# A two-layer attention and mixture-of-experts trunk: the first norm's scale and shift moved onto turned rows, pass 0 fed by a product, the expert choice rewritten

## The chip, the cores and the metric

The kernel runs on one core of one Trainium2 chip. The metric is the device time of one execution in microseconds (us). The kernel before took 848.21 us, the median of three runs (848.0 to 849.41).

The core has a matrix engine (PE; its weight loads are shown apart as PEld), a vector engine (DVE), a scalar engine (ACT), GpSimd (POOL), and a queue (SP) that issues most of the DMA transfers. Every engine works through its own list of instructions in order, and waits on semaphores for the others.

## What is computed

512 tokens of width 1024 pass through two layers. Each layer computes an attention part and an output projection, adds the residual, and norms (the first norm); then a router picks two of 16 experts for each token, within one of four groups, and the result of the experts is added and normed again. What matters here is the stretch from the first norm to the experts:

```python
x = layer_norm(DEEPNORM_ALPHA * x + einsum('bsm,md->bsd', mix, w_out[l]), ln1_g[l], ln1_b[l])

def moe_ffn(x, w_router, router_bias, w_gate, w_up, w_down):
    scores = sigmoid(dot(xt, w_router))
    biased = (scores + router_bias).reshape(N, N_GROUPS, EXPERTS_PER_GROUP)     # 4 groups of 4
    group_score = sum(top_k(biased, 2)[0], axis=-1)
    g_sel = argmax(group_score, axis=-1)
    in_group = take_along_axis(biased, g_sel[:, None, None], axis=1)[:, 0]
    _, local = top_k(in_group, 2)
    expert_idx = g_sel[:, None] * EXPERTS_PER_GROUP + local
    w = take_along_axis(scores, expert_idx, axis=1);  w = w / sum(w, axis=-1, keepdims=True)
    gates = sum(one_hot(expert_idx, N_EXPERTS) * w[..., None], axis=1)
    h = silu(einsum('nd,edf->enf', xt, w_gate)) * einsum('nd,edf->enf', xt, w_up)
    return einsum('enf,efd->nd', h * gates.T[:, :, None], w_down)

x = layer_norm(DEEPNORM_ALPHA * x + moe_ffn(x, ...), ln2_g[l], ln2_b[l])
```

## The kernel before

**Who sets the order.** The program is written as many small streams (Python generators, functions whose names begin with `s_`) that a planner, `Flow`, interleaves when the program is built. Each step names an engine and an estimated cost; the planner takes the step that can start first, with a small weight for the stream's priority (`PRIO`). What it fixes is the order of each engine's list. At run time an engine only waits for the data of the next instruction in its list.

**The stretch at stake.** The 512 tokens are four tiles, t = 0 to 3, of 128 rows, held in `X`. The output projection (`s_wout`; its products are L283 to L285) ends with tile 3. For each half tile `s_half` adds the residual and takes statistics (L970, L972). `s_router` turns the tile with PE (L441), ACT copies it (L279), PE multiplies it by the router's weights (L1035), and three small DVE steps make the logits (L1041, L1045, L1046). `s_norm1` applies the norm to `X` with four DVE instructions of 512 columns a tile (two at L990, two at L998), with mean, deviation, gain and shift, and then SP stores the tile in DRAM (`XD`, L1060). `s_choose` works on a pair of tiles (q = 0: tiles 0 and 1; q = 1: tiles 2 and 3): ACT's exponential (L1070), then a chain of small DVE steps from L1080 on (comparisons of all pairs in a group, the best group, ties) that ends in the one-hot choice `ohb` (L1098). `s_rank` counts with PE (L1188 to L1191) at which place of its expert's list each token stands, and builds from that on DVE the operands of one more product (L1195 to L1212). That product, `s_table` (L1221), gives for each pass and slot the row to fetch; DVE writes it as integers (L1225).

**Passes.** Each expert has room for 96 tokens. The 16 x 96 slots are cut into 12 passes of 128. For a pass, POOL gathers its 128 rows from `XD` by an indirect DMA (`s_gather`, L1293), PE turns them with eight transposes (`turn_rows`, L1505), ACT and DVE copy the turned rows out of the banks in two pieces of 512 columns (`s_rows`, through L279 and L280), and PE multiplies them by gate and up weights (`s_passes`, L1596; four products of 32 slots side by side). ACT and DVE make the hidden values (`s_act`, L1474, L1475), PE turns them (L1502) and multiplies them by the down weights (`second`, L1570). Weights are loaded by SP (L1355, L1357, L1361) into slots that the passes set free. All of this is in float32; the trace shows two records for each float32 product that isn't a transpose (64 at L1596 for the 32 of a pass).

**Filler.** From the end of the projection until the planner thinks that the first gather has landed, `s_warm` puts products of a matrix of ones into PE's list (L1124); their result isn't used.

**The end of a layer.** The last two passes stay on chip (`NEAR`); the others' rows go to DRAM and come back (`s_far`). `s_combine` adds them to alpha times `X` and norms. For tiles 0 and 2, `s_alpha` multiplies `X` by alpha on ACT (L1620); for tiles 1 and 3 a product with `ident_alpha` does it (L1675).

Of the kernel before, what the change touches and what calls it, by code (L numbers as in the profile page):

```python
# [6 lines left out]
F32 = mybir.dt.float32  # L7
# [9 lines left out]
P = 128  # L17
D = 1024
# [16 lines left out]
FAR = 8192.0  # L35

# [159 lines left out]
def body(tc, sb, pp, dr, x, w_in, attn_sinks, c_q_norm_g, c_kv_norm_g, w_uq, w_ukv, w_out, ln1_g, ln1_b,  # L196
# [105 lines left out]
    ident_alpha = fixed(P)  # L302
    V.tensor_scalar(ident_alpha, ident, ALPHA, None, op0=OP.mult)
# [16 lines left out]
    desc = fixed(4)  # L320
    V.tensor_scalar(desc, iotf[:, :4], -1.0, float(NE), op0=OP.mult, op1=OP.add)
    lower = fixed(4, 4)
    G.iota(lower, pattern=[[1, 4], [-1, 4]], base=0, channel_multiplier=0, allow_small_or_imprecise_dtypes=True)
    V.tensor_scalar(lower, lower, 0.0, None, op0=OP.is_gt)
# [45 lines left out]
    for key, n in (("sg", 2 * NE), ("zz", 2 * NE), ("bi", 2 * NE), ("c1", 8 * NE), ("c2", 8 * NE), ("g4", 2 * NE), ("rk", 2 * NE), ("gs", 8), ("m1", 8),  # L370
                   ("pick", 8), ("oh", 4 * NE), ("wts", 4), ("posk", 4), ("row", 4), ("eb", 4), ("op", 4 * NP)):
# [107 lines left out]
    def layer(l, xready, prev_free):  # L479
# [542 lines left out]
        def s_router(t):  # L1022
            yield E("gain")
            r0, z = smalls["r0", t], smalls["zz", t // 2][:, t % 2 * NE:(t % 2 + 1) * NE]
            for h in range(2):
# [17 lines left out]
            yield E("stat", t)  # L1043
            mv, rs = smalls["mv", t], smalls["rs", t]
            yield ve(16, lambda: V.scalar_tensor_tensor(r0, gbv[:, 0], mv[:, 0:1], r0, op0=OP.mult, op1=OP.subtract))  # L1045
            e = yield ve(16, lambda: V.scalar_tensor_tensor(z, r0, rs[:, 0:1], gbv[:, 1], op0=OP.mult, op1=OP.subtract))  # L1046
# [8 lines left out]
        def s_norm1(t):  # L1055
            yield E("gb1")
            er = yield E("stat", t)
            e = yield from s_norm(t, (aux.of(F32), gb1), E("stat", t).got, er, None, True)
            flow.set(E("normed", t), e)
            xd = yield dma(524e3, lambda: SY.dma_start(XD[l][t * P:(t + 1) * P, :], X[:, t]), [e])  # L1060
            flow.set(E("xd", t), xd)


        def s_choose(q):
# [5 lines left out]
            t = yield ac(32, lambda: A.activation(sg, smalls["zz", q], AF.Exp), [flow.now])  # L1070
            flow.set(E("exp", q), t)
            C1, C2 = (c.rearrange("p (g a b) -> p g a b", a=4, b=4) for c in (c1, c2))
            b84, G84, R84 = (a.rearrange("p (g a) -> p g a", a=4) for a in (bi, g4, rk))
            other = b84[:, :, None, :].to_broadcast([P, 8, 4, 4])
            own = b84[:, :, :, None].to_broadcast([P, 8, 4, 4])
            gs2, pick2 = (a.rearrange("p (t g) -> p t g", t=2) for a in (gs, pick))

            def v(fn, after=None):
                return ve(60, fn, after)
            yield v(lambda: V.tensor_scalar(sg, sg, 1.0, None, op0=OP.add))  # L1080
# [698 lines left out]
```

## Time and profile before

| | us |
|---|---|
| median of three runs | 848.21 |
| profiled execution, its own time | 847.3 |
| profiled execution, its span | 845.5 |
| PE busy in it | 817.0 (97%) |
| DVE busy | 510.3 (60%) |
| ACT busy | 315.4 (37%) |
| POOL busy | 103.6 (12%) |

The span runs from the first instruction to the last; the 1.8 us around it belong to the execution's own time. Busy time of PE contains the filler products, so it doesn't tell by itself how much of the work of PE is needed. The granted clock of PE was 0.996 over the whole span.

### The profile page before, as it was taken

What the parts mean: (1) busy time and instruction counts of PE and PEld (TensorE: products, weight loads), DVE (VectorE), ACT (ScalarE), POOL (GpSimd) and SP (SyncE); (2) the same over time, 40 slices, a digit from 0 to 9 for tenths busy, and PEclk for the clock granted to TensorE, in tenths of its full rate; (3) what the DMA queues carried; (4) which work ended last, traced back from release to release, by engine and by line L of the source; (5) the groups of instructions that cost most, each with busy time, mean ns of one, the idle gap of its engine ahead of it and who ended that gap; (6) DMA issues with size and microseconds to landing.
All of it is one profiled execution on the core that took longest, in us unless ns stands there. A gap on an engine that the chain in (4) does not pass through costs nothing. (4 is left out here: it accounts for less than half of the span.)

```text
span 845.5 us, 16062 instructions
## 1 busy us (share of the span) xinstructions
PE 817.0 (97%) x6288; PEld 534.9 (63%) x6288; DVE 510.3 (60%) x1504; ACT 315.4 (37%) x790; POOL 103.6 (12%) x135
## 2 busy tenths in 40 slices
PE   7999999999999999999999999999999999999995
PEld 7878896667896333333587889776688843333332
DVE  6799999975591130002998999999458513100157
ACT  4434647973111222122245174677531112212211
POOL 1010102000002111100211001200101111111004
PEclk9999999999999999999999999999999999999998
DMA  8422340174476999997444218010944579999862
GB/s 267 149 79 80 114 169 26 26 258 140 151 275 187 340 373 376 370 362 284 163 105 143 75 51 273 2 52 26 338 160 163 188 272 365 373 367 367 293 270 100
DMA packets 119138, 172.73 MB, mean 204 GB/s; under 512 B 12101, under 2 KB 95557, under 8 KB 119056
## 3 DMA queue, kind: packets, MB, share of 16 engines
q1 hardware_dynamic: 112720, 156.12, 54.1%
q0 software_dynamic: 6336, 15.52, 5.2%
q8 instruction: 51, 0.84, 0.4%
q14 instruction: 31, 0.25, 0.1%
HBM read 154.01 MB, written 25.17 MB: 212 GB/s over the span
## 5 line engine op out<-in xcount | busy, mean ns | idle before, releaser
L283 PE MATMUL bank<-ring,ra 128*128 128x512 f32 (+4 forms) x448 | 167.1, 373 | 0.5 <-ACT fa L605 0.5
L1596 PE MATMUL bank<-fa,ra 128*32 128x512 f32 x1080 | 159.7, 592 | 1.2 <-DVE ra L280 0.7
L284 PE MATMUL bank<-ring,xl 128*128 128x512 f32 (+4 forms) x448 | 157.5, 352 | 0.9 <-DVE xl L452 0.9
L285 PE MATMUL bank<-ring,ra 128*128 128x512 f32 (+4 forms) x448 | 157.9, 352 | 0.0
L279 ACT ACTIVATE fa<-bank 128x512 f32<-128x512 f32 (+3 forms) x170 | 85.5, 517 | 142.5 <-PE bank L441 82.6
L1475 DVE TENSOR_TENSOR fa<-fa,bank 128x256 f32<-128x256 f32 x24 | 10.1, 420 | 200.3 <-ACT fa L1474 200.3
L1596 PEld LDWEIGHTS bank<-fa,ra 128*32 128x32 f32 x1080 | 49.8, 110 | 75.5 <-issue 70.1
L283 PEld LDWEIGHTS bank<-ring,ra 128*128 128x128 f32 x448 | 85.0, 190 | 14.8 <-issue 7.1
L285 PEld LDWEIGHTS bank<-ring,ra 128*128 128x128 f32 x448 | 84.8, 189 | 8.2
L284 PEld LDWEIGHTS bank<-ring,xl 128*128 128x128 f32 x448 | 85.2, 190 | 7.4 <-DVE xl L452 1.3
L1570 PE MATMUL bank<-fa 128*32 128x512 f32 x504 | 80.4, 595 | 1.5 <-DVE fa L280 0.6
L441 PE MATMUL bank<-fa 128*128 128x128 f32 (+1 forms) x456 | 71.5, 281 | 7.4 <-DMA fa<-in_x_dram 5.7
L441 PEld LDWEIGHTS bank<-fa 128*128 128x128 f32 (+1 forms) x456 | 55.1, 143 | 24.4 <-issue 10.5
L474 ACT ACTIVATE ring<-fa 128x1024 fp32r<-128x1024 f32 (+4 forms) x56 | 49.4, 897 | 56.1 <-PE bank L284 49.8
L1596 PE MATMUL bank<-ring,ra 128*32 128x512 f32 x360 | 67.1, 592 | 0.0
L1474 ACT ACTIVATE fa<-bank 128x256 f32<-128x256 f32 x24 | 9.2, 385 | 151.7 <-PE bank L1596 151.7
L475 DVE TENSOR_TENSOR ring<-fa,ring 128x1024 fp32r<-128x1024 f32 (+4 forms) x56 | 58.4, 1051 | 7.8 <-ACT ring L474 7.8
L747 DVE MATCH_REPLACE8 aux<-fa,aux 128x256 f32<-128x256 f32 (+2 forms) x96 | 51.8, 544 | 0.0
L746 DVE MAX8 fa<-aux 128x8 f32<-128x256 f32 (+2 forms) x96 | 50.6, 550 | 0.1
L787 PE MATMUL bank<-fa 64*128 64x256 f32 (+7 forms) x256 | 47.4, 413 | 0.0
L800 ACT ACTIVATE fa<-fa 128x256 f32<-128x256 f32 (+3 forms) x89 | 44.5, 503 | 0.0
L1570 PEld LDWEIGHTS bank<-fa 128*32 128x32 f32 x504 | 19.3, 108 | 35.6 <-issue 34.1
(222 smaller groups left out, 1221.2 us busy)
## 6 DMA issues: line engine op xcount, KB each, us to landing
fa<-in_w_gate_dram SPq DMA_DIRECT2D x45, 512.0 KB
fa<-in_w_up_dram SPq DMA_DIRECT2D x45, 512.0 KB
fa<-in_w_down_dram SPq DMA_DIRECT2D x21, 1024.0 KB
xl<-in_w_down_dram SPq DMA_DIRECT2D x9, 1024.0 KB
fa<-in_w_out_dram SPq DMA_DIRECT2D x8, 1024.0 KB
yd<-fa SPq DMA_DIRECT2D x16, 512.0 KB
ring<-in_w_gate_dram SPq DMA_DIRECT2D x15, 512.0 KB
ring<-in_w_up_dram SPq DMA_DIRECT2D x15, 512.0 KB
```

Of the source, the lines that this page charges most:

```text
L279: return Step([("A", 0.05 + n / 1200, lambda: A.activation(dst, src, AF.Copy)), ("V", 0.12 + n / 960, lambda: V.tensor_copy(dst, src))], a ...
L283: T.matmul(ps, xh, wh, start=start, stop=False)
L284: T.matmul(ps, xl, wh, start=False, stop=False)
L285: T.matmul(ps, xh, wl, start=False, stop=stop)
L441: T.transpose(ps[:n, j, :], s, ident)
L474: yield Step([("A", 0.09 + n / 1200, lambda: A.activation(hv, raw, AF.Copy))], None)
L475: t = yield ve(n, lambda: V.tensor_tensor(lv, raw, hv.bitcast(F32), op=OP.subtract))
L746: yield ve(nk, lambda: V.max(m8, sc))
L747: yield ve(nk, lambda: V.match_replace(sc, m8, sc, MARK))
L787: T.matmul(got[1][:, a * nk:(a + 1) * nk], qs[h], ks[h], start=True, stop=True)
L1570: T.matmul(a[1][cs], ht[:, j, cs], E("raw", e, 2).got[1][:, j, n * 512:(n + 1) * 512], start=j == 0, stop=j == 1)
L1596: T.matmul(acc[1][cs], gh[:, 4 * u + j, cs], E("raw", e, u).got[1][:, j], start=u + j == 0, stop=u + j == 4)
```

## The change

1. **The norm is split.** `s_norm1` now only subtracts the mean and divides by the deviation, in one ACT instruction of 1024 columns a tile. Gain and shift (`gcol`, already there by column for the router) are applied where the rows are turned: `s_rows` copies each of the eight turned blocks of 128 columns with one ACT or DVE instruction that multiplies by the gain and adds the shift. Blocks were copied four at a time before.
2. **Pass 0 by a product.** `s_first` builds for each tile a 128 x 128 matrix that holds a one where a token belongs to a slot of pass 0, and multiplies `X` by it. The sum over the four tiles is the turned rows of pass 0, so pass 0 has no gather and no transposes. `s_warm` fills only until the last of these matrices is there.
3. **The choice by differences.** `s_choose` subtracts all pairs and compares the differences with 0 or with a tiny negative number, once for experts and once for groups. A token that finds no room gets a large place number (`NONE`) in `s_rank`.
4. **The logits.** The two halves of a tile's logits are joined in one DVE step that reads the bank.
5. **The residual's share put late.** `X` needs alpha times gain and shift for the end of the layer. `s_alpha` now does that for all four tiles with four DVE instructions of 512 columns each, after `first`, `table` and the store of the tile. `ident_alpha` becomes `ident`.

The core of the diff (left out: constants, the overflow branch, names):

```diff
@@ s_router
                 else:
-                    e = yield ve(16, lambda: V.tensor_tensor(r0, r0, gp[1][:, :NE], op=OP.add))
+                    tp = e
+                    es = yield E("stat", t)
+                    mv, rs = smalls["mv", t], smalls["rs", t]
+                    e = yield ve(16, lambda: V.scalar_tensor_tensor(r0, gbv[:, 0], mv[:, 0:1], r0, op0=OP.mult, op1=OP.subtract), [es])
+                    e = yield ve(16, lambda: V.scalar_tensor_tensor(r0, r0, rs[:, 0:1], gbv[:, 1], op0=OP.mult, op1=OP.subtract), [e])
+                    e = yield ve(16, lambda: V.scalar_tensor_tensor(z, gp[1][:, :NE], rs[:, 0:1], r0, op0=OP.mult, op1=OP.subtract), [e, tp])
@@ s_norm1
-            yield E("gb1")
             er = yield E("stat", t)
-            e = yield from s_norm(t, (aux.of(F32), gb1), E("stat", t).got, er, None, True)
+            for h in range(2):
+                yield E("seen", h, t)
+            mv, rs = smalls["mv", t], smalls["rs", t]
+            e = yield ve(1, lambda: V.tensor_scalar(rs[:, 1:2], mv[:, 0:1], rs[:, 0:1], -1.0, op0=OP.mult, op1=OP.mult), [er])
+            e = yield ac(D, lambda: A.activation(X[:, t], X[:, t], AF.Identity, scale=rs[:, 0:1], bias=rs[:, 1:2]), [e])
             flow.set(E("normed", t), e)
             xd = yield dma(524e3, lambda: SY.dma_start(XD[l][t * P:(t + 1) * P, :], X[:, t]), [e])
+        def s_alpha(t):
+            yield E("gb1")
+            yield E("first")
+            yield E("table")
+            yield E("xd", t)
+            g, b = aux.of(F32), gb1
+            for h in range(2):
+                cs = slice(h * 512, (h + 1) * 512)
+                yield ve(512, lambda: V.scalar_tensor_tensor(X[:, t, cs], X[:, t, cs], ALPHA, g[:, cs], op0=OP.mult, op1=OP.mult))
+                e = yield ve(512, lambda: V.scalar_tensor_tensor(X[:, t, cs], b[:, cs], ALPHA, X[:, t, cs], op0=OP.mult, op1=OP.add))
@@ s_warm
-            while E("gathered").t is None or flow.free["T"] < E("gathered").t:
+            while E("warm").t is None or flow.free["T"] < E("warm").t:
                 e = yield pe(0.22, f, [])
+        def s_first():
+            for t in range(NT):
+                yield E("posk", t // 2)
+                yield E("normed", t)
+                yield E("stat", NT - 1)
...
+                yield v_small(lambda: V.tensor_scalar(m[:, t], iotf, pos[0], None, op0=OP.is_equal), [])
+                te = yield v_small(lambda: V.scalar_tensor_tensor(m[:, t], iotf, pos[1], m[:, t], op0=OP.is_equal, op1=OP.add))
+                if t == NT - 1:
+                    flow.set(E("warm"), te)
+                def f():
+                    for k in range(KD):
+                        T.matmul(banks_[k // 4][1][:, k % 4 * P:(k % 4 + 1) * P], X[:, t, k * P:(k + 1) * P], m[:, t], start=t == 0 and k % 4 == 0,
+                                 stop=t == NT - 1 and k % 4 == 3)
+                yield E("logits", NT - 1)
+                te = yield pe(0.214 * KD, f, [te])
@@ s_rows
-            for h in range(2):
-                t = yield from turned(banks_[h], banks_[h][1].rearrange("p (a b) -> p a b", b=P), te, E("gt", p).got[0][:, 4 * h:4 * h + 4])
+            for k in range(KD):
+                dst, src = E("gt", p).got[0][:, k], banks_[k // 4][1][:, k % 4 * P:(k % 4 + 1) * P]
+                g, b = gcol[:, 0, k:k + 1], gcol[:, 1, k:k + 1]
+                t = yield Step([("A", 0.42, lambda: A.activation(dst, src, AF.Identity, scale=g, bias=b)),
+                                ("V", 0.33, lambda: V.tensor_scalar(dst, src, g, b, op0=OP.mult, op1=OP.add))], [te])
@@ s_passes and the gathers
-            yield from turn_rows(None, 0, GT)
+            te = yield E("first")
+            gt = yield Take(GT)
+            E("gt", 0).got = (rshape(gt[1], KD, P), gt)
+            flow.go(B0 + PRIO["experts"] - 20, s_rows(0, E("first").got, te))
-        for p in range(NP):
+        for p in range(1, NP):
             flow.go(B0 + PRIO["experts"], s_gather(p))
@@ s_combine
-                        T.matmul(ps, ident_alpha, xt[:, cs], start=True, stop=False)
+                        T.matmul(ps, ident, xt[:, cs], start=True, stop=False)
```

What this does to the engines' lists, at two places of the first layer (the second layer has the same). First PE, from the counting products of tiles 2 and 3 to the first pass. Before, fillers (L1124) stand on both sides of the table's 16 products, then the eight transposes of the gathered rows (L1505, from `fa`, where the gather writes), then pass 0:

```order
L1124 LDWEIGHTS ones
L1124 MATMUL bank_68<-ones 128x128
L1505 MATMUL bank_73<-fa 128x128 x4
L1505 MATMUL bank_67<-fa 128x128 x4
L1596 MATMUL bank_72<-fa,ra_2148 32x512 x32
```

With the change 28 fillers (now L1133) are followed by the products of tiles 2 and 3 (L1247), and the table (now L1262) stands behind them:

```order
L1133 LDWEIGHTS ones
L1133 MATMUL bank_73<-ones 128x128
L1247 MATMUL bank_68<-fa 128x128 x4
L1247 MATMUL bank_66<-fa 128x128 x4
L1247 MATMUL bank_68<-fa 128x128 x4
L1247 MATMUL bank_66<-fa 128x128 x4
L1262 LDWEIGHTS sl_105
```

After the table four fillers follow, and then pass 0 (L1648). The same products of tiles 0 and 1 stand ahead of the counting products of tiles 2 and 3, behind 44 fillers in three groups; 76 fillers remain in the layer where 296 stood.

Second DVE, at the end of the choice for tiles 2 and 3. Before, the last part of the norm (L998) stands right ahead of the step that writes `ohb`, and twelve steps of the other pair's rank (L1200 to L1212) are mixed in; from L1080 to `ohb` it is 29 instructions. The end of it:

```order
L1095 TENSOR_REDUCE fa<-fa 128x2
L1212 TENSOR_TENSOR rv_115<-fa 128x4x24
L1096 TENSOR_TENSOR fa<-fa 128x8
L998 SCALAR_TENSOR_TENSOR fa<-fa 128x512
L1098 SCALAR_TENSOR_TENSOR ohb<-fa 128x32
L1104 SCALAR_TENSOR_TENSOR fa<-fa 128x32 x2
L1106 TENSOR_TENSOR fa<-fa 128x64
L1107 TENSOR_REDUCE fa<-fa 128x4
L1195 TENSOR_TENSOR fa<-fa,bank_73 128x64
```

With the change no instruction of 512 columns is left in this chain; from the choice's first step (L1103) to `ohb` (L1112) it is 21 instructions, and the last of them are:

```order
L1108 TENSOR_REDUCE fa<-fa 128x8
L1061 TENSOR_SCALAR fa<-fa 128x1
L1099 TENSOR_TENSOR fa<-fa 128x32
L1101 TENSOR_TENSOR fa<-fa 128x32
L1102 TENSOR_REDUCE fa<-fa 128x8
L1111 SCALAR_TENSOR_TENSOR fa<-fa 128x32
L1112 TENSOR_SCALAR ohb<-fa 128x32
```

Third DVE, after the first pass's copies. Before, the copies of passes 0 and 1 followed the gates directly. With the change sixteen instructions of `s_alpha` (L1076, L1077) stand there, fifteen of them ahead of the first pass's hidden values (L1524):

```order
L1076 SCALAR_TENSOR_TENSOR fa<-fa,aux_119 128x512 x2
L1077 SCALAR_TENSOR_TENSOR fa<-fa 128x512 x2
L1076 SCALAR_TENSOR_TENSOR fa<-fa,aux_119 128x512
L1524 TENSOR_TENSOR fa<-fa,bank_72 128x256
L1077 SCALAR_TENSOR_TENSOR fa<-fa 128x512
```

Behind the first pass both engines' lists are otherwise the same as before, but for the eight smaller copies a pass. On SP's list the store of tile 2 moves ahead of three weight loads; on POOL's one gather a layer is gone.

## Rows read from the trace of the kernel before

**Rows 1.** The page's head: span, and engines with busy time, share, instructions
```profile
span 845.5 us, 16062 instructions
PE 817.0 (97%) x6288; PEld 534.9 (63%) x6288; DVE 510.3 (60%) x1504; ACT 315.4 (37%) x790; POOL 103.6 (12%) x135
```

**Rows 2.** Timeline of PE, layer 0: start us, us, instruction, count, [idle before <-releaser]
```profile
239.37 1.74 PE L1124 MATMUL bank<-ones 128*128 128x128 bf16 x28
...
242.29 1.07 PE L1035 MATMUL bank<-fa 128*128 128x16 f32 x8 [0.17 <-ACT fa L279]
...
250.16 0.17 PE L1191 MATMUL bank<-ohb,before 128*128 128x16 bf16 x1 [0.26 <-DVE ohb L1098]
...
250.31 3.06 PE L1124 MATMUL bank<-ones 128*128 128x128 bf16 x52
253.22 0.70 PE L1221 MATMUL bank<-rv,sl 128*128 128x24 bf16 x16
...
259.48 1.09 PE L1505 MATMUL bank<-fa 128*128 128x128 f32 x8 [0.32 <-DMA fa<-xd,ti]
260.83 7.16 PE L1596 MATMUL bank<-fa,ra 128*32 128x512 f32 x64 [0.25 <-ACT ra L279]
...
269.36 0.62 PE L1596 MATMUL bank<-fa,ra 128*32 128x512 f32 x2 [0.35 <-DVE ra L280]
```

**Rows 3.** The same view of layer 1: its first filler and its pass 0
```profile
651.98 1.74 PE L1124 MATMUL bank<-ones 128*128 128x128 bf16 x28
...
673.68 7.16 PE L1596 MATMUL bank<-fa,ra 128*32 128x512 f32 x64 [0.25 <-ACT ra L279]
```

**Rows 4.** Timeline of DVE, layer 0
```profile
245.36 0.18 DVE L1080 TENSOR_SCALAR fa<-fa 128x32 f32<-128x32 f32 x1
...
249.26 0.74 DVE L998 SCALAR_TENSOR_TENSOR fa<-fa 128x512 f32<-128x512 f32 x1
249.93 0.18 DVE L1098 SCALAR_TENSOR_TENSOR ohb<-fa 128x32 bf16<-128x32 f32 x1
...
250.99 0.22 DVE L1198 TENSOR_REDUCE fa<-fa 128x4 f32<-128x64 f32 x1
251.25 0.16 DVE L1200 TENSOR_TENSOR fa<-fa 128x4 f32<-128x4 f32 x1
...
253.95 0.18 DVE L1225 TENSOR_SCALAR ti<-bank 128x24 int32<-128x24 f32 x1 [0.41 <-PE bank L1221]
...
255.67 0.21 DVE L1147 TENSOR_TENSOR fa<-fa 128x48 f32<-128x48 f32 x1
...
278.35 0.35 DVE L1167 SCALAR_TENSOR_TENSOR fa<-sl,fa 128x128 f32<-128x128 bf16 x1
```

**Rows 5.** Timeline of POOL, layer 0: the gathers of pass 0 and of a later pass
```profile
255.02 1.26 POOL L1293 DMA_INDIRECT fa<-xd,ti  x1 [12.89 <-DVE fa L1144]
...
278.05 0.99 POOL L1293 DMA_INDIRECT fa<-xd,ti  x1 [7.78 <-DMA fa<-in_w_gate_dram]
```

**Rows 6.** Timeline of SP's queue, layer 0: the store of tile 3, the next weight load
```profile
250.04 0.34 SPq L1060 DMA_DIRECT2D xd<-fa  x1
264.52 0.37 SPq L1355 DMA_DIRECT2D fa<-in_w_gate_dram  x1
```

**Rows 7.** Timeline of ACT, layer 0: the exponential of tiles 2 and 3
```profile
244.69 0.23 ACT L1070 ACTIVATE fa<-fa 128x32 f32<-128x32 f32 x1 [2.45 <-DVE fa L1046]
```

**Rows 8.** Timeline of PE: 24 float32 records of an attention product, 128 columns or paired
```profile
143.98 2.57 PE L787 MATMUL bank<-fa 96*128 96x128 f32 x24
```

**Rows 9.** Groups by line and shape: count | busy us, mean ns | idle before
```profile
L1647 DVE SCALAR_TENSOR_TENSOR fa<-xl,fa 128x512 f32<-128x512 f32 x8 | 5.8, 746 | 0.1
...
L810 ACT ACTIVATE ring<-ring,fa 128x128 f32<-128x128 f32 x7 | 2.5, 394 | 0.5 <-DVE fa L805 0.5
```

**Rows 10.** A stretch of layer 0: length, busy PE, PEld, DVE, ACT, POOL, granted clock, DMA share, GB/s
```profile
260.80:400.00 139.20, 137.77 (x1240) 50.60 (x1240) 22.10 (x52) 31.32 (x60) 19.09 (x19) 1.00 0.97 337
```

**Rows 11.** Waits of SP's queue, 200 to 420 us: line, releaser, us, times, longest
```profile
SPq L1355 <- PE bank L1596: 28.9, 7, 14.1
```

More of the change, by code (lines that the diff above doesn't have):

```diff
@@ L35 @@
 FAR = 8192.0
+TINY = 1.5e-38
+NONE = 4096.0
 class Event:
@@ L1073, in s_choose, with beaten @@
             b84, G84, R84 = (a.rearrange("p (g a) -> p g a", a=4) for a in (bi, g4, rk))
[L1074 to L1076 removed]
+            gs2 = gs.rearrange("p (t g) -> p t g", t=2)
             def v(fn, after=None):
                 return ve(60, fn, after)
+            def beaten(c, vals, n, left):
+                yield v(lambda: V.tensor_tensor(c, vals[:, :, None, :].to_broadcast([P, n, 4, 4]), vals[:, :, :, None].to_broadcast([P, n, 4, 4]),
+                                                op=OP.subtract))
+                yield v(lambda: V.tensor_tensor(c, c, beats[:, None].to_broadcast([P, n, 4, 4]), op=OP.is_gt))
+                yield v(lambda: V.tensor_reduce(left, c, axis=AX.X, op=OP.add))
@@ L1155, in s_near @@
             for t in range(NT):
-                yield E("normed", t)
+                yield E("alpha", t)
             yield E("gu", 2)
@@ L1213, in s_rank @@
             flow.set(E("rank", q), e)
+        def s_first():
+            for t in range(NT):
+                yield E("posk", t // 2)
+                yield E("normed", t)
+                yield E("stat", NT - 1)
+                if t == 0:
+                    gm = yield Take(WT)
+                    m = rshape(gm[1], NT, P)
+                    banks_ = yield Take(PS, 2)
+                pos = [smalls["posk", t // 2][:, 2 * k + t % 2:2 * k + t % 2 + 1] for k in range(2)]
+                yield v_small(lambda: V.tensor_scalar(m[:, t], iotf, pos[0], None, op0=OP.is_equal), [])
[8 more added lines that the diff above has]
+                te = yield pe(0.214 * KD, f, [te])
+            WT.put(gm, te)
+            E("first").got = banks_
+            flow.set(E("first"), te)
+        flow.go(B0 + 62.9, s_first())
         def v_small(fn, after=None):
@@ L1399, in overflow @@
                                 T.transpose(pb[:, j], g[:, (4 * b + j) * P:(4 * b + j + 1) * P], ident)
-                            A.copy(gt[:, 4 * b:4 * b + 4], pb)
+                            for j in range(4):
+                                A.activation(gt[:, 4 * b + j], pb[:, j], AF.Identity, scale=gcol[:, 0, 4 * b + j:4 * b + j + 1],
+                                             bias=gcol[:, 1, 4 * b + j:4 * b + j + 1])
                         for u in range(2):
@@ L1634, in s_far @@
             if SUM[l][t] == 2:
+                yield E("alpha", t)
                 gw = yield Take(YO)
```

91 lines of the change are left out of this document (36 added, 55 removed).

## The prediction, made before the changed kernel ran

> **What bounds the kernel now.** I read the page's head first [rows 1]. PE is busy for 97% of the span, DVE for 60%, ACT for 37%. That looks like a kernel bound by PE, but filler products count as busy. So I read PE's timeline next, from the projection's last product on. In layer 0 the first filler starts at 239.37 us and pass 0 at 260.83 [rows 2]; in layer 1 at 651.98 and 673.68 [rows 3]. These two stretches of 21.46 and 21.70 us hold little needed work: turning the last tile, its router product (1.07), the counting products, the table (0.70), eight transposes (1.09). What sets their length is a chain through other engines, and that chain is what the change rewrites.
>
> The chain in layer 0: the router's product of tile 3 ends at 243.36 (242.29 + 1.07) [rows 2]. DVE's choice starts at 245.36 and writes the one-hot rows at 249.93, that is 4.57 us for 29 instructions, with a norm instruction of 0.74 us directly ahead of the last [rows 4]. PE answers 0.26 after that with the counting products, and fillers follow from 250.31 [rows 2]. DVE builds the table's operands, the table runs at 253.22, and DVE writes the rows' numbers at 253.95 [rows 2, 4]. POOL gathers at 255.02 [rows 5], and the rows are in the core at 259.48, 4.46 later [rows 2]. Then transposes, a copy, and pass 0. The store of the tile that the gather reads is issued at 250.04 [rows 6], so the gather starts 4.98 after the store and 1.07 after the number is written; the store may well be what ends last there.
>
> **The choice.** The exponential starts at 244.69 [rows 7], 1.33 after the router's product, with three DVE steps between. One step remains, and no norm instruction stands in DVE's way. A handoff of 0.26, a step of about 0.2, the exponential's 0.23 and a handoff back give a start of the choice at about 244.1 instead of 245.36. It then has 21 instructions to the one-hot rows. The price of one: before, (4.57 - 0.67) / 28 = 0.14 where steps of two streams alternate, and 0.26 where each waits for the one ahead (250.99 to 251.25) [rows 4]. With less to alternate with I take 0.18, 3.6 us; the bounds are 0.14 (2.9) and the old 4.57. One-hot rows: 247.7, within 247.0 to 248.7. PE meanwhile has the products of tiles 0 and 1, which end at about 247.6 (below), so an earlier one-hot is worth no more than some tenths.
>
> **The products for pass 0.** Each tile adds eight float32 products of 128 columns, 16 records. The trace of before doesn't have them. Nearest are an attention product with 24 records in 2.57, 0.107 each [rows 8], and the router's and transposes' eight records in 1.07 and 1.09, 0.134 to 0.136 each [rows 2]. So a tile costs 1.7 to 2.2; I take 1.9, nearer to the first since that has the same kind of operands and twice-recorded products too. Tiles 0 and 1 go where fillers stood, beside the choice: from 243.36 with eight fillers to about 247.6. Tiles 2 and 3 are on the path.
>
> Sum for layer 0 after the one-hot rows at 247.7: 0.26 to PE, and the counting products, to about 248.3. DVE's few steps from the counts to the place numbers and the first matrix (six at 0.2 to 0.26) end at 249.6 to 249.9. 28 fillers at 3.06 / 52 = 0.059 [rows 2] last 1.65, to 249.95, so the fillers cover these steps. Two tiles at 1.9: 253.75. Table 0.65 to 0.70, four fillers 0.23: pass 0 at **254.5**. For the table's operands DVE went from its second step on the counts at 250.99 [rows 4] to the table's start at 253.22 [rows 2], 2.2 us; from 248.8 on, with up to four matrix steps of 0.35 among them, they are there by 252.4, ahead of PE. The copies of the eight blocks start when the products end at 253.75. The first takes 0.35 to 0.39 by the nearest rows [rows 4, 9] and a handoff of 0.26, 254.4, beside the table; the two engines then deliver blocks faster than pass 0 uses them.
>
> Layer 0 gains 260.83 - 254.5 = 6.3. With the cheaper steps and products it is 7.3 (0.7 and 0.4 less, of which 0.1 is lost to PE's own work), with the dearer 4.7 (1.0 and 0.6 more). Layer 1 has the same list and a stretch 0.24 longer; I take 6.5.
>
> **What I cost at nothing, and its cover.** *The norm:* sixteen DVE instructions of about 0.75 a layer go, twelve us; four ACT instructions of 1024 columns come. ACT's rows have 128 columns in 0.394 [rows 9], so one lies between 0.4 and 3.15; the store of tile 3, whose statistics precede the router's logits, is then issued at 247.8 at the latest instead of 250.04. The next gather, of pass 1, follows the table at about 255.4. Even at the old 4.98 between store and gather it would be free at 252.8.
>
> *Pass 1's rows:* gather at 255.4 and 4.46 to land, 259.9. Pass 0 ends at 254.5 + 7.16 = 261.7. Margin 1.8; if the margin goes, pass 1 waits.
>
> *Alpha:* fifteen DVE instructions of 512 columns at 0.746 [rows 9], 11.2 us, now stand ahead of pass 0's hidden values. They follow the gates, which ended at 255.88, 1.93 after the table's number [rows 4], so now at about 256.5; the train ends at 267.7. Before, pass 1 starts at 269.36 [rows 2] and with 7.16 ends at 276.5; only then PE wants the hidden values of pass 0. Moved by 6.3 this is 270.2. Margin 2.5. If that cover is gone, the excess is paid once a layer.
>
> *Eight small copies a pass:* three on ACT at 0.39 and five on DVE at 0.35, 1.8 us beside each other, where two of 512 were. They lie beside PE's down products in all passes but 0 and 1. At pass 1 PE waits 0.35 now [rows 2]; it may become 0 or 0.7.
>
> **Does an earlier pass 0 stay earned?** Behind pass 0 PE is busy for 137.77 of 139.20 us, but the DMA engines are at 97% too, at 337 GB/s [rows 10]. If the weights' stream had its own pace, PE would wait at pass 2 or 3 for what it gained. Against that: SP issues no weight load between the store at 250.04 and 264.52 [rows 6], because it waits for slots that PE sets free; its waits on pass products are 28.9 us in seven, one of 14.1 [rows 11]. The slots are full when pass 0 starts, so the stream's next load moves with pass 0. The idle 14 us of the stream shrink, and the time behind moves as a whole.
>
> **Rivals.** *The wait moves to pass 1's gather.* For it: the margin is 1.8 only, POOL's first gather took 1.26 against 0.99 for a later one [rows 5], and three gathers queue behind each other. A landing 3 to 5 us later makes 1.2 to 3.2 a layer: 837.8 to 841.8.
>
> *DVE's alpha train locks GpSimd out.* POOL writes the descriptors of its gathers itself, and the train's instructions read two operands from the core's memory for 11.2 us without a pause. If the gather of pass 1 waited for the train's end, it would land at 267.7 + 4.46 = 272.2, 10.5 after pass 0's end; 10.5 - 6.4 = 4.1 a layer lost, 848.2 + 8.2 = 856.4. It decides against the change from a hold of 8.2 us (margin 1.8 plus gain 6.4). Against it: the gather at 278.05 took 0.99 with a DVE instruction of two operands running from 278.35 [rows 4, 5], and by the order this gather's issue is not behind the train but a microsecond ahead. For it: the gather at 255.02, with small DVE steps beside it, did take 1.26.
>
> The Trainium skill, page "SBUF — State Buffer", section on the two separate sides, has this as a rule: a VectorE instruction with two inputs in SBUF, against a GpSimd one that reads SBUF, takes the port pair that the two share for its whole length, and the other blocks; descriptors from the POOL queue then starve. By that rule POOL would get in at the latest between two instructions of the train, 0.75 us each, or, if it loses each time, only at its end. The trace agrees at most in the 0.27 us more of the first gather.
>
> *The weights' stream has its own pace,* and pass 0's gain is given back within the layer: 848.2, no change. For it the 97% of [rows 10], against it the waits in [rows 11].
>
> **How the numbers follow.** The profiled execution took 847.3: 845.5 of span [rows 1] and 1.8 around it. The gain is 6.3 + 6.5 = 12.8, so 834.5 by the profile, and on the median of 848.21, 0.9 above it, **835.4**. Own range: 7.3 + 7.5 gives 833.4, 4.7 + 4.9 gives 838.6. Chances: forecast 0.71, pass 1's gather 0.15, own pace 0.06, lock 0.08. The range for 8 in 10 takes the own range and the first rival's, a little wider at the low end for the tenth or two of pass 1: 833.0 to 842.0. About 0.2% (1.7 us) is what a measurement of this kernel can tell from no change; faster by more are the forecast and the first rival, 0.86; within it the own pace and a lock near its deciding point, 0.06; slower 0.08.
>
> **What would show it.** On PE's timeline of the changed kernel pass 0 should start some 6.4 us nearer to the first filler, 15.1 us instead of 21.5, with 76 fillers; the products of a tile should take 1.7 to 2.2; choice to one-hot rows 2.9 to 4.6. Pass 1 should start 8.5 us behind pass 0 as now; if PE waits there for DMA, it is the first rival, and if POOL's gather stretches while the train runs, the second. If PE's idle time between pass 2 and the layer's end grows by some 6 us with DMA named, the stream has its own pace. A layer end that moves by less than pass 0 would make the sum wrong in a place I haven't named.

## The result, and the profile after

The changed kernel took 834.13 us, the median of four runs (832.55 to 836.23). The kernel before took 848.81 beside it; the ratio is 0.9834, with a 95% interval of 0.9812 to 0.9857. The forecast was 835.4, the range 833.0 to 842.0. Two later sets of runs gave 834.62 and 833.99 for the same kernel, against 847.89 and 846.76 for the one before. So the gain is 12.8 to 14.7 us, where 12.8 was forecast. Two executions of the runs below took far longer than the others of their kernel (3972.59 us in e1_oldnorm, 1164.67 in e2_bybank) and are left out of the medians.

The profiled execution of the changed kernel took 835.47, its span is 833.7. These are the rows on the page that answer to [rows 1]: of 6288 records on PE 5960 are left, and DVE has more busy time than before, not less: by the groups of its lines the norm takes some 24 us away, alpha brings 21.0, and the copies by blocks take 41.8 where the turned rows took 15.1.

```profile
span 833.7 us, 15557 instructions
PE 806.0 (97%) x5960; PEld 521.7 (63%) x5960; DVE 537.5 (64%) x1588; ACT 338.2 (41%) x852; POOL 103.2 (12%) x133
```

PE's timeline of the two stretches answers to [rows 2, 3] (start us, us, instruction, count, idle before and its releaser):

```profile
239.89 1.51 PE L1133 MATMUL bank<-ones 128*128 128x128 bf16 x24
...
244.25 3.84 PE L1247 MATMUL bank<-fa 128*128 128x128 f32 x32
...
248.43 1.72 PE L1133 MATMUL bank<-ones 128*128 128x128 bf16 x28
250.31 3.84 PE L1247 MATMUL bank<-fa 128*128 128x128 f32 x32
253.98 0.55 PE L1262 MATMUL bank<-rv,sl 128*128 128x24 bf16 x16
...
254.70 3.65 PE L1648 MATMUL bank<-fa,ra 128*32 128x512 f32 x32
...
262.86 0.33 PE L1554 MATMUL bank<-fa 128*128 128x128 f32 x1 [0.73 <-DMA fa<-xd,ti]
...
646.85 1.51 PE L1133 MATMUL bank<-ones 128*128 128x128 bf16 x24
...
661.67 3.65 PE L1648 MATMUL bank<-fa,ra 128*32 128x512 f32 x32
...
669.02 1.09 PE L1554 MATMUL bank<-fa 128*128 128x128 f32 x8
```

From the first filler to pass 0 it is now 14.81 us in layer 0 (254.70 - 239.89) and 14.82 in layer 1 (661.67 - 646.85), where it was 21.46 and 21.70. What is new in the first layer is the wait of 0.73 for the gather of pass 1, ahead of its transposes; layer 1 doesn't have it.

DVE's timeline answers to [rows 4]:

```profile
244.43 0.18 DVE L1103 TENSOR_SCALAR fa<-fa 128x32 f32<-128x32 f32 x1
...
248.05 0.18 DVE L1112 TENSOR_SCALAR ohb<-fa 128x32 bf16<-128x32 f32 x1
...
249.90 0.35 DVE L1241 SCALAR_TENSOR_TENSOR fa<-fa 128x128 f32<-128x128 f32 x1
...
253.29 0.41 DVE L1514 TENSOR_SCALAR ra<-bank,fa 128x128 f32<-128x128 f32 x1 [1.09 <-PE bank L1247]
254.23 0.73 DVE L1514 TENSOR_SCALAR ra<-bank,fa 128x128 f32<-128x128 f32 x2 [0.53 <-ACT ra L1513]
255.52 0.73 DVE L1514 TENSOR_SCALAR ra<-bank,fa 128x128 f32<-128x128 f32 x2 [0.56 <-ACT ra L1513]
256.16 0.18 DVE L1266 TENSOR_SCALAR ti<-bank 128x24 int32<-128x24 f32 x1
...
257.61 1.29 DVE L1076 SCALAR_TENSOR_TENSOR fa<-fa,aux 128x512 f32<-128x512 f32 x2
...
266.28 0.69 DVE L1076 SCALAR_TENSOR_TENSOR fa<-fa,aux 128x512 f32<-128x512 f32 x1
266.88 0.42 DVE L1524 TENSOR_TENSOR fa<-fa,bank 128x256 f32<-128x256 f32 x1
267.21 0.69 DVE L1077 SCALAR_TENSOR_TENSOR fa<-fa 128x512 f32<-128x512 f32 x1
```

The choice takes 3.62 us to the one-hot rows (244.43 to 248.05). L1241 writes the matrix of tile 2, for which PE's products at 250.31 wait. The eight copies of pass 0 run from 253.29 to past 256: DVE waits for ACT between its copies (0.53, 0.56), and ACT for DVE, and the step that writes the table's numbers (L1266) stands behind them, 2.2 us after the table began. The page's group of these copies says how general that is (count, busy us and mean ns of one, idle before and its releaser):

```profile
L1514 DVE TENSOR_SCALAR ra<-bank,fa 128x128 f32<-128x128 f32 x110 | 41.8, 408 | 27.9 <-ACT ra L1513 24.5
```

POOL answers to [rows 5]:

```profile
257.22 1.26 POOL L1334 DMA_INDIRECT fa<-xd,ti  x1 [14.55 <-DVE fa L1153]
...
264.22 3.61 POOL L1334 DMA_INDIRECT fa<-xd,ti  x1 [3.14 <-PE bank L1554]
```

The first of these is the gather of pass 1, now at 257.22; its rows are there at 262.86, or just ahead. The second took 3.61 us where such a gather took 0.99 before. It ends at 267.83. The sixteen alpha instructions that follow one another on DVE (the train, as the prediction calls them) run until 267.90 (267.21 + 0.69); one instruction of another kind, the hidden values at 266.88, stands ahead of the last of them.

### The profile page after: what moved, and what is told of

Read it like the earlier page. It is cut to its first block, busy times and chain, and to the rows that moved or that the text cites. A ratio compares the mean times of both kernels' runs of the same rounds, so it can differ in the third digit from the quotient of the medians.

```text
span 833.7 us, 15557 instructions
## 1 busy us (share of the span) xinstructions
PE 806.0 (97%) x5960; PEld 521.7 (63%) x5960; DVE 537.5 (64%) x1588; ACT 338.2 (41%) x852; POOL 103.2 (12%) x133
## 5 line engine op out<-in xcount | busy, mean ns | idle before, releaser
L1648 PE MATMUL bank<-fa,ra 128*32 128x512 f32 x1080 | 160.0, 592 | 0.2
L281 ACT ACTIVATE fa<-bank 128x256 f32<-128x256 f32 (+3 forms) x172 | 86.1, 514 | 108.2 <-PE bank L440 80.2
L1524 DVE TENSOR_TENSOR fa<-fa,bank 128x256 f32<-128x256 f32 x24 | 10.1, 421 | 160.3 <-ACT fa L1523 160.3
L1648 PEld LDWEIGHTS bank<-fa,ra 128*32 128x32 f32 x1080 | 47.6, 109 | 76.6 <-issue 65.6
L1648 PE MATMUL bank<-ring,ra 128*32 128x512 f32 x360 | 67.1, 592 | 0.0
L1514 DVE TENSOR_SCALAR ra<-bank,fa 128x128 f32<-128x128 f32 x110 | 41.8, 408 | 27.9 <-ACT ra L1513 24.5
L1513 ACT ACTIVATE ra<-bank,fa 128x128 f32<-128x128 f32 x82 | 33.7, 458 | 41.1 <-DVE ra L1514 36.6
```

The lines of the kernel that those rows point to most:

```text
L281: return Step([("A", 0.05 + n / 1200, lambda: A.activation(dst, src, AF.Copy)), ("V", 0.12 + n / 960, lambda: V.tensor_copy(dst, src))], a ...
L1648: T.matmul(acc[1][cs], gh[:, 4 * u + j, cs], E("raw", e, u).got[1][:, j], start=u + j == 0, stop=u + j == 4)
```

## The experiments

All were made on the changed kernel. "Gap" is the time from the projection's end (the first filler) to pass 0, 14.81 us in the changed kernel.

**Which part gave what.** Part 2 undone: pass 0 is gathered again.

```diff
-            te = yield E("first")
-            gt = yield Take(GT)
...
+            yield from turn_rows(None, 0, GT)
-        for p in range(1, NP):
+        for p in range(NP):
             flow.go(B0 + PRIO["experts"], s_gather(p))
```

(left out: the products themselves go, the fillers last until the gather, and alpha waits for it)

> The changed kernel with pass 0 gathered and turned again (part 2 of the change undone, all else kept). Theory (the gain is the chain to pass 0, and most of it is the gather that pass 0 no longer waits for): one-hot rows stay at about 8.2 us behind the projection's end, the table comes some 2 us earlier than with products, then number, gather, 4.5 us to land, transposes: pass 0 at about 20 us behind the projection instead of 14.8, so +5 a layer, 843 to 845. Rival (the gain is mostly the shorter choice and norm on DVE, and the products give back what the gather took): pass 0 within 2 us of the changed kernel's, 834 to 838.

845.0 us (843.31 to 845.89), ratio to before 0.9962 (0.9947 to 0.9977). PE's rows of layer 0:

```profile
239.59 1.51 PE L1133 MATMUL bank<-ones 128*128 128x128 bf16 x24
...
257.90 1.09 PE L1555 MATMUL bank<-fa 128*128 128x128 f32 x8 [1.03 <-DMA fa<-xd,ti]
259.10 7.16 PE L1646 MATMUL bank<-fa,ra 128*32 128x512 f32 x64
```

The gap is 19.51 (259.10 - 239.59), 4.7 more than with products, in each layer. The rival, that the products give back what the gather took, falls. Without the products the rest of the change shortens the gap by some 2 us a layer (21.46 to 19.51).

Part 3 undone, the choice as before:

```diff
-            yield from beaten(C1, b84, 8, R84)
+            yield v(lambda: V.tensor_tensor(C1, other, own, op=OP.is_ge))
+            yield v(lambda: V.tensor_tensor(C2, other, own, op=OP.is_gt))
+            yield v(lambda: V.tensor_tensor(C1, C1, lower[:, None, :, :].to_broadcast([P, 8, 4, 4]), op=OP.mult))
+            yield v(lambda: V.tensor_tensor(C1, C1, C2, op=OP.max))
...
```

> The changed kernel with the expert choice written as before (part 3 undone: 16 steps of the choice's own to the one-hot rows instead of 13, and one more behind them). Theory: three or four dependent DVE steps of 0.2 us, so pass 0 some 0.6 to 0.9 later a layer, 835 to 836 where the changed kernel has 834. Rival (the choice is what shortened the chain): 2 us a layer, 838.

835.67 (835.5 to 837.76), 1.05 more than the changed kernel on the same chip; pass 0 starts 0.76 later (a gap of 15.57) in both layers. The new choice is worth that and no more.

Parts 1 and 5 undone:

```diff
-            e = yield ac(D, lambda: A.activation(X[:, t], X[:, t], AF.Identity, scale=rs[:, 0:1], bias=rs[:, 1:2]), [e])
+            e = yield from s_norm(t, (aux.of(F32), gb1), E("stat", t).got, er, None, True)
...
-            for h in range(2):
...
+            e = yield ac(D, lambda: A.activation(X[:, t], X[:, t], AF.Copy, scale=ALPHA))
```

(left out: the turned rows are copied without gain and shift)

> The changed kernel with gain and shift applied in the norm again, on DVE, plain copies of the turned rows, and alpha by one ACT instruction a tile (parts 1 and 5 undone). Three norm instructions of 512 columns then stand among the choice's last steps on DVE, 0.65 to 0.75 each. Theory: one-hot rows and pass 0 2.0 us later a layer, 838. Rival (PE's products of tiles 0 and 1 and the fillers cover the norm): within 0.5 us a layer, 834 to 835. No train of alpha instructions runs on DVE here; if that train holds GpSimd's gathers, they are at 1.0 to 1.3 us in this kernel, and the one that took 3.61 isn't there.

837.34 (836.86 to 838.24), ratio 0.9875 (0.9858 to 0.9892). The same kernel once more, for its trace:

> The kernel of e1_oldnorm again, for its trace: gain and shift in the norm on DVE, plain copies, alpha on ACT. It took 837.4 where the changed kernel took 834.6. Expected: pass 0 some 1.4 us later in each layer than in the changed kernel (16.2 us behind the projection's end instead of 14.8), the one-hot rows later by the three norm instructions of 0.67 each less what the waits between dependent steps left free; gathers on GpSimd at 1.0 to 1.3 us.

837.64, a single execution. DVE at the end of the choice, and PE's pass 0:

```profile
247.85 0.74 DVE L989 SCALAR_TENSOR_TENSOR fa<-fa,aux 128x512 f32<-128x512 f32 x1
248.51 0.17 DVE L1095 TENSOR_REDUCE fa<-fa 128x8 f32<-128x32 f32 x1
248.61 0.74 DVE L997 SCALAR_TENSOR_TENSOR fa<-fa 128x512 f32<-128x512 f32 x1
249.27 0.18 DVE L1104 SCALAR_TENSOR_TENSOR fa<-fa 128x32 f32<-128x32 f32 x1
249.37 0.74 DVE L997 SCALAR_TENSOR_TENSOR fa<-fa 128x512 f32<-128x512 f32 x1
250.03 0.17 DVE L1105 TENSOR_SCALAR ohb<-fa 128x32 bf16<-128x32 f32 x1
```

Three norm instructions stand ahead of the one-hot rows, and pass 0 starts at 256.68, a gap of 16.84: 2.03 later than in the changed kernel, as e1_oldnorm's theory had it, and more than the 1.4 that e3_oldnorm expected from the time. The time is only 2.7 to 3.7 us longer, not 4.1; part of the rest comes back behind pass 0: pass 1 starts 8.66 behind it in layer 0 where e3_again has 9.11, and the pass phases are 0.2 to 0.3 shorter in each layer. All gathers on POOL are at 0.99 to 1.26 us here.

Undone one by one, the parts cost 10.4 + 1.05 + 2.7 = 14.15 us, and the whole is 13.3 on that chip. So the product for pass 0 is about three quarters. In the gaps the parts overlap more: 4.7 + 0.76 + 2.03 = 7.5 a layer against 6.65 for the whole. Part 4, the logits, was not undone. The choice starts 5.99 us behind the first filler before (245.36 - 239.37), 4.54 with the change and 4.88 with the old norm (244.72 in e3_oldnorm); how much of that is due to the logits and how much to the order of DVE's list was not tried apart.

**What a tile's products cost, and whether the gain reaches the end.**

```diff
                     for k in range(KD):
+                        if t >= 2:
+                            T.matmul(banks_[k // 4][1][:, k % 4 * P:(k % 4 + 1) * P], X[:, t, k * P:(k + 1) * P], maskC[:, :P], start=False, stop=False)
```

> The changed kernel with each product of tiles 2 and 3 that feeds pass 0 preceded by one with a matrix of zeros, which adds nothing: 32 more records a layer. Theory (the products of two tiles are on the path with 1.84 to 1.92 us a tile, and what pass 0 loses or gains reaches the end): pass 0 starts 3.7 to 3.8 us later in each layer, and the time is 7.5 us more, 841 to 842.5. Rival (the weights' stream has its own pace and gives back or absorbs what pass 0 gains or loses): less than half of it, 834 to 838.

840.73 (839.03 to 842.92), 6.1 more than the changed kernel had in the set before (834.62), 6.6 more than e2_latealpha beside it (834.15), whose pass 0 is at the same place. Pass 0 starts 3.35 later in both layers, not 3.75. PE's rows of layer 0:

```profile
248.27 1.72 PE L1133 MATMUL bank<-ones 128*128 128x128 bf16 x28
249.83 0.44 PE L1248 MATMUL bank<-fa 128*128 128x128 f32 x2
...
257.17 0.55 PE L1264 MATMUL bank<-rv,sl 128*128 128x24 bf16 x16
```

The 64 records take 7.34 us (249.83 to 257.17), exactly twice the 3.67 of the 32 in the changed kernel (250.31 to 253.98), so the price of a tile, 1.84, is confirmed. The missing 0.32 lies ahead of them. The zero products need no matrix from DVE and start 1.56 us behind the first of the 28 fillers; in the changed kernel the products start 1.88 behind it (250.31 - 248.43). So there PE waits some 0.3 us for the matrix of tile 2 (ready at 249.90 + 0.35 = 250.25), which the fillers don't quite cover. 2 x 3.35 = 6.7 arrive as 6.1 to 6.6: what pass 0 loses or gains does reach the end, and the theory stands.

**The late gather of pass 1.**

```diff
-            for k in range(KD):
+            for k in (0, 4, 1, 5, 2, 6, 3, 7):
...
-                t = yield Step([("A", 0.42, lambda: A.activation(dst, src, AF.Identity, scale=g, bias=b)),
+                t = yield Step([("A", 0.42, lambda: A.activation(dst, src, AF.Identity, scale=g, bias=b)) if k >= 4 else
```

> The changed kernel with the eight block copies of a pass split by bank: DVE copies the four blocks of one bank, ACT the four of the other. In the changed kernel the two engines take turns within each bank and wait for each other, so pass 0's eight copies take 3.0 us and the step that writes the table's numbers stands behind them on DVE, 2.2 us after the table. Theory (those turns are why pass 1's gather is late in layer 0): copies in about 1.5 us, numbers 1.2 to 1.6 us earlier, pass 1's gather as much earlier, and PE's wait of 0.2 to 0.7 us ahead of pass 1 in layer 0 is gone; 833.5 to 834.5. Rival (the landing is set by the store of the tile or by DMA): the wait stays.

841.73 (839.67 to 844.57), ratio 0.994 (0.992 to 0.996): 7 to 8 us worse than the changed kernel, and neither theory said so. The rows show that both the first theory and a mistake of the edit are true. DVE, then PE:

```profile
251.63 1.37 DVE L1515 TENSOR_SCALAR ra<-bank,fa 128x128 f32<-128x128 f32 x4 [1.10 <-PE bank L1247]
252.91 0.18 DVE L1266 TENSOR_SCALAR ti<-bank 128x24 int32<-128x24 f32 x1
...
264.84 1.04 DVE L1515 TENSOR_SCALAR ra<-bank,fa 128x128 f32<-128x128 f32 x3
```

```profile
260.14 1.09 PE L1556 MATMUL bank<-fa 128*128 128x128 f32 x8
264.38 0.62 PE L1650 MATMUL bank<-fa,ra 128*32 128x512 f32 x2 [3.14 <-DVE ra L1515]
...
673.30 10.12 PE L1650 MATMUL bank<-fa,ra 128*32 128x512 f32 x64 [3.28 <-DVE ra L1515]
```

Four copies on one bank take 1.37 us without a wait, the table's number is written at once, and PE doesn't wait for pass 1's gather in either layer. But the DVE half of pass 1's copies now stands behind the alpha train and comes at 263.9 and 264.84; PE waits 3.1 to 3.3 us for it, in both layers. Pass 1 so starts 11.26 and 11.39 behind pass 0, where e3_again has 9.11 and 8.56. In layer 1 the wait has a second price: pass 1 takes 10.05 us to the next transposes (673.30 to 683.35) instead of 7.23, at a granted clock of 0.71 by the view of the stretches (its numbers are explained at the fillers, below); in layer 0, after a wait of 3.14, the clock stayed at 1.00.

```profile
673.30:683.40 10.10, 10.10 (x65) 4.56 (x65) 1.50 (x4) 0.00 (x0) 0.00 (x0) 0.71 0.42 147
```

Later starts and slower clock add up to 7.8 (2.15 + 2.83 + 2.82). In the changed kernel the planner gave all eight copies of pass 1 to ACT. The prediction's remark that the train has a cover of 2.5 us at the hidden values is not the whole truth: the copies of pass 1 have none, and only ACT saves them.

To take away that mistake, alpha was held back as well:

```diff
-            yield E("first")
-            yield E("table")
+            yield E("gu", 2)
             yield E("xd", t)
```

(with the copies by bank: e3_best; with them as in the changed kernel: e2_latealpha)

> The changed kernel with the sixteen alpha instructions held back until pass 2's gate and up products, behind the copies of pass 3. Theory (the train on DVE holds GpSimd's gathers only now and then, and none on the path): the gathers that run beside the train in the changed kernel (1.1 to 3.6 us there) take 1.0 here, and the time is the same within 1 us, 833.5 to 835. Rival (the train delays the landing of pass 1's rows: 4.9 to 5.3 us in layer 0 against 4.46 before the change): landing at 4.5 or less, no wait of PE at pass 1, 833 to 834.

834.15 (832.99 to 835.35): no change. The gathers beside pass 1 take 0.99 on POOL, as expected of a kernel with no train there. From the gather's start to the transposes it is still 5.07 us in layer 0 (255.77 to 260.84), and PE waits 0.17. So the train isn't why the rows land later than after the 4.46 of before.

```profile
255.77 1.26 POOL L1333 DMA_INDIRECT fa<-xd,ti  x1 [14.56 <-DVE fa L1152]
260.84 1.09 PE L1553 MATMUL bank<-fa 128*128 128x128 f32 x8 [0.17 <-DMA fa<-xd,ti]
```

> The changed kernel with the copies of every pass split by bank and the alpha instructions held back until pass 2's gate and up products, behind pass 3's copies, so that no copy on DVE stands behind the train. Theory: e2_bybank lost 6.4 us because its DVE half of pass 1's copies stood behind the train on DVE; without the train there that loss is gone, pass 1's gather starts some 1.9 us earlier than in the changed kernel (as in e2_bybank) and PE waits neither for it nor for the copies: the changed kernel's time less 0.2 to 1.0, 833 to 834.4. Rival (the split itself costs the time): 838 or more.

> The changed kernel once more, unchanged, beside e3_best on the same chip: 833.5 to 835.5. PE's wait for pass 1's gather in layer 0 was 0.73 us in its first trace and 0.23 in the second; expected between 0.2 and 0.8 again.

836.34 against 833.99 for the unchanged kernel on the same chip: 2.3 us worse, against the theory. The gather starts 1.6 us earlier than in e3_again, not 1.9 (15.75 and 17.33 behind the first filler). Pass 1 starts 8.45 us behind pass 0 in both layers, as meant (9.11 and 8.56 in e3_again, with a wait of 0.48 in layer 0). The loss is somewhere else. At the start of layer 1 the planner's order now has PE wait 3.24 us for DVE's copies of L451; in e3_again the first of these holds PE for 0.92 (the two rows are of e3_best and of e3_again):

```profile
419.61 0.63 PE L440 MATMUL bank<-fa 128*128 128x128 f32 x4 [3.24 <-DVE xl L451]
...
418.49 0.42 PE L286 MATMUL bank<-ring,xl 128*128 128x324 f32 x1 [0.92 <-DVE xl L451]
```

That is 2.3 more, and behind the wait the granted clock falls here too (0.80 from 419.60 to 428.00). From pass 0 of layer 0 to the first filler of layer 1 e3_best takes 2.6 us longer than e3_again (394.48 against 391.91). So the copies by bank do what they should, and an order that the planner makes elsewhere takes more back. No version here beats the changed kernel.

**Does the train lock GpSimd out?** The gates were put behind the train, so that pass 1's gather is issued in the middle of it:

```diff
             yield E("oh", q)
-            yield E("table")
+            yield E("alpha", NT - 1)
```

> The changed kernel with the gates' steps put behind the sixteen alpha instructions, so that the train starts on DVE right after the table's numbers, and pass 1's gather is issued in the middle of it instead of just ahead. Rival of the prediction (the train locks GpSimd out until its end): the gather's instruction takes up to 9 us, its rows land some 10 us late, PE waits for them at pass 1, up to 9 us a layer, 843 to 853. Theory (GpSimd gets in between two instructions): the instruction takes 1.0 to 1.9 us and the time is 834 to 836.

836.01 (834.22 to 836.59), at the upper edge of the theory. POOL's gather of pass 1, layers 0 and 1:

```profile
256.37 1.44 POOL L1334 DMA_INDIRECT fa<-xd,ti  x1 [14.55 <-DVE fa L1076]
...
663.42 1.37 POOL L1334 DMA_INDIRECT fa<-xd,ti  x1 [14.48 <-DVE fa L1076]
```

0.2 us more than ahead of the train, and PE's wait for the rows is 0.88 and 0.48. The rival's 9 us are not there. But long holds do occur: in e3_best a scatter was issued in the middle of its train (271.40 to 281.1) and took

```profile
275.05 6.95 POOL L1338 DMA_INDIRECT yd<-fa,ti  x1 [3.29 <-ACT fa L281]
```

with its end at 282.0, 0.9 behind the train's. The traces have eight such instructions of more than 2 us: 3.61 (above), 4.91 (e1_gathered), 2.60 and 3.01 (in this run, the gather behind those of passes 1 to 3), 2.42 and 2.56 (e2_bybank), 6.95 and 6.89 (e3_best). Each ended 0.86 to 0.90 us behind an alpha instruction after which DVE paused or went on with the hidden values, which read a bank; above that is 266.28 + 0.69 = 266.97 and the gather's end at 267.83. Others beside such trains took 0.99 to 1.49, and what decides between the two isn't shown. PE shows no wait for the eight. The Trainium skill, page "SBUF — State Buffer", section on the two separate sides, has the ports that the two engines share as a lock: for a vector instruction with two inputs in SBUF, against a GpSimd one that reads SBUF, whichever starts first holds them for its whole instruction and the other blocks. The trace agrees that POOL is blocked, and goes further: at times it doesn't get in between the instructions of a train at all, for up to 6.95 us. Of descriptors that starve, which the prediction took from that section too, the page speaks for vector instructions in a two-port mode; no run here tells by which of the two POOL was held.

**The fillers.**

```diff
-        flow.go(B0 + 150, s_warm())
```

> The changed kernel without any filler product: 76 products of ones a layer less, PE idle in their place for 4.7 us in five pieces. Theory (the chain on DVE sets the time, and the fillers only keep PE busy): pass 0 at the same place if the granted clock stays at 2.4 GHz, 834 to 835. Rival (PE's clock falls in the idle pieces): the products of tiles 2 and 3, the table and the first pass run at 1.2 GHz for a while, 3.8 us more for the two tiles alone, 838 to 845, and the granted clock of that stretch shows it.

836.53 (835.3 to 838.56), 2.5 more. Measured from the projection's last product, pass 0 of layer 0 starts 0.66 earlier than with fillers, at a granted clock of 1.00, and that of layer 1 starts 3.24 later. The granted clock is the number behind the five busy times, here of the stretch with the products of tiles 0 and 1 in each layer (the stretches aren't of one length):

```profile
242.00:247.00 5.00, 4.25 (x40) 4.17 (x40) 4.50 (x28) 2.91 (x4) 0.00 (x0) 1.00 1.04 407
...
650.00:658.00 8.00, 8.00 (x49) 7.99 (x49) 5.12 (x30) 2.91 (x4) 0.37 (x1) 0.57 1.06 395
```

0.57 is the lower of the two levels for most of the stretch; the same 32 records took 6.67 us there, against 3.84. PE had idle pieces of 0.78 and 0.75 just ahead, in both layers. So the rival came true in one layer out of two. Where the clock held, nothing was won either: pass 0 came 0.66 earlier, but PE then waited 1.18 us for pass 1's gather, whose transposes start 22.98 us behind the projection's last product, against 22.69 to 23.20 in the three traces with fillers.

**The unchanged kernel once more.**

> The changed kernel once more, unchanged, beside the kernels that undo one part each, to have its time and its trace from the same chip. Expected: 833 to 836. In its first trace pass 0 of layer 0 starts 14.8 us behind the projection and PE then waits 0.73 us for the gather of pass 1 in layer 0 and not at all in layer 1; whether that wait comes again is what is looked at.

834.62 (833.23 to 835.17). The gaps are 14.81 in layer 0 and 14.80 in layer 1, the wait for pass 1's gather 0.23 in layer 0, none in layer 1.

## Why the prediction was right, by its steps

**The gap.** Forecast 15.1, measured 14.8. The choice was to start 4.7 us behind the projection and take 3.6 us; it started after 4.54 and took 3.62. Two tiles of products were to take 3.8; from the first record to the table it is 3.67 (250.31 to 253.98). The 28 fillers were to cover DVE's steps and nearly did: by e2_twice PE waits some 0.3 us for the matrix of tile 2 behind them. Table and four fillers took 0.72, not 0.9. Every term was within 0.25 us. The written terms add up to 254.65 and not to the 254.5 of the forecast (253.75 + 0.65 to 0.70 + 0.23), so by them the gap was forecast 15.3, and 0.45 of small differences, most of them to the good, lie between.

**The copies of pass 0** were mis-sized: 1.8 us beside each other were forecast, 3.0 measured (253.29 to 255.52 + 0.73). For the 1.8 only the durations of single copies stood. The engines share a bank and take turns in it, with waits that the kernel's own code doesn't name; with one bank for each engine they are gone (e2_bybank). The Trainium skill, page "PSUM — Partial Sum Buffer", section "PSUM bank collisions raise a hardware error", states that two engines in one bank at once raise an error and aren't made to wait by the hardware. No run here lets them. That blocks come faster than pass 0 uses them held all the same (eight in 3.0 us, for products of 7.2), and PE shows no wait there. The step that failed is another: that the gather of pass 1 "follows the table at about 255.4". The step that writes the table's numbers stands on DVE behind five of the copies, and the prediction gave that no time. In the traces of before, of the changed kernel, of e2_bybank and of e2_trainfirst the gather starts 0.9 us behind the end of this step (in the changed kernel 257.22 behind 256.34), whatever the time since the store of the tile; so it is the number, not the store that the prediction suspected, that it waits for.

**The first rival,** the wait that moves to pass 1's gather, came true in small. The gather starts at 257.22 instead of 255.4, 1.8 late, which alone would just not be felt, since pass 0 ends at 262.12 and not at 261.7 (257.22 + 4.46 is 261.7). The wait is 0.73, 0.23 and 0.48 in layer 0 in three traces of the kernel, and 0 in layer 1. It comes from the second part: from the gather's start to the transposes it is 5.1 to 5.6 us there instead of 4.46. Neither the store, issued 8.6 us ahead of the gather (248.60), nor the train (e2_latealpha) is the cause. In the changed kernel a weight load is issued at 258.40, in the middle of the gather's flight, where before none was under way. By itself it doesn't explain the delay either: in layer 1 of e3_again such a load comes 1.25 us behind the gather (664.51 and 663.26), and the trace has the rows landed 4.5 us after its start. The cause stays open.

**What was costed at nothing** was so for the norm and for the hidden values (266.88 on DVE, wanted by PE at 271.17). The store of tile 3 was to be issued at 247.8 at the latest and came at 248.60, without harm. That the train ends at 267.9, where 267.7 was forecast, is luck: it began 1.1 us late (257.61, not 256.5), and its instructions follow each other every 0.6 us, not 0.746, so that the fifteen of the forecast end at 266.97 already.

**The stream's own pace** is no cause that gives the gain back. From the transposes of the first pass's hidden values to those of the last it is 122.75 us before and 122.79 after in layer 0, 123.20 and 123.51 in layer 1; in e3_again it is 122.79 and 122.86, in e1_again 123.61 and 124.29. So one of the later passes is late now and then, by up to 1.7 us in a layer, of which a wait of 0.72 for `in_w_up` is shown in e1_again's layer 1. That the moved passes come nearer to the stream there, and that some scatter between runs is from it, is likely and not shown.

**The sum.** Between the two profiled executions pass 0 of layer 0 moved by 6.13, pass 1 by 5.30, pass 0 of layer 1 by 12.01 and the span by 11.8. The forecast of 6.3 and 6.5 a layer holds for the gaps (6.65 and 6.88); 0.5 was lost ahead of layer 0's stretch, 0.4 of it in the first 75 us, which the change doesn't touch, 0.8 between passes 0 and 1 of layer 0, and 0.3 in the passes of layer 1. That the total came so near to the forecast is in part two errors of opposite sign: the gaps gave 13.5 and not 12.8, and pass 1's wait took some of it back.

## What to carry to other kernels

Where a chain through DMA decides (number, gather, landing, turning: 7 us here), a product with a selection matrix may do the same work on PE for 1.8 us a tile, and half of the tiles can lie beside the chain that chooses. When a wait is removed, look at the step that stands behind the new work on the same engine: here the table's numbers behind five copies. Two engines that empty one bank together were slower here (3.0 us) than with one bank each (1.4 and 1.5), but a fixed split needs both engines free.

## What the runs showed of the hardware

GpSimd's indirect DMA instructions took 1.0 to 1.5 us beside a train of two-input DVE instructions in most cases, and 2.4 to 6.95 in eight; all eight ended 0.86 to 0.90 us behind an alpha instruction that was followed by a pause or by one that reads a bank. Without fillers PE's clock fell to the lower level in one layer (0.57 granted over 8 us) and not in the other, with idle pieces of less than a microsecond in both. Behind a single wait of some 3 us it fell in layer 1 of e2_bybank (3.28 us, 0.71 granted over the 10 us behind it) and didn't in layer 0 (3.14 us, 1.00).
